# Dummy products ahead of the first transposes, 256-column key-value products and weight splitting on GpSimd in a hybrid decoder layer

## The chip, the cores and the metric

The kernel runs on one core of one Trainium2 chip. The metric is device time in microseconds, from the start to the end of one execution. A core has five engines with queues of their own: TensorE (PE, with its weight loads as PEld), VectorE (DVE), ScalarE (ACT), GpSimd (POOL) and SyncE (SP), which here only issues DMAs. PE multiplies from the on-chip memory SBUF into the eight banks of PSUM.

## The reference

One decoder layer on x of 1024 rows and 1024 columns, all in float32:

```
h  = rms_norm(x, pre_g);  z = h @ w_in            # 1024 x 7184
qa, ka, va, ga, qb, kb, vb, gb, gk_low = split(z)
oa = (softmax(q1 k1^T) - lam * softmax(q2 k2^T)) @ va     # 8 heads, causal
oa = rms_norm(oa, subln_g) * 0.8 * silu(ga)
ob = gated linear attention(qb, kb, vb, gk_low)           # 4 groups, chunks
ob = rms_norm(ob, gla_g) * silu(gb)
out = x + rms_norm(concat(oa, ob) @ w_out, post_g)
```

## The kernel before, in words

**Split products.** A large product runs on float32r operands: each is split into a high part, rounded by an ACT copy into a float32r tile, and a low part, the rest, subtracted by DVE. Three matmuls (high x high, low x high, high x low) make up one product. The linear attention's products of keys, values and state use plain float32 tiles.

**Start.** SP loads x in tiles of 128 rows. For tiles 0 to 3, `norm_x` (L486) squares a tile on ACT, makes the reciprocal root with `rstd` (L1477) on ACT and DVE, and scales the first 512 columns on DVE (L482) and the others on GpSimd. `first(0)` (L529) transposes the first halves on PE (L120) and `put` (L519) splits the result into high parts `h_hi` (ACT, L521) and low parts `h_lo` (DVE, L522); GpSimd adds them back as `f1` (L542). `first(1)` does the same for the second halves. `blocks` (L550) transposes rows 512 to 1023 (tiles 4 to 7, normalised in two groups of two) and forms the sums and differences s1 to s4 of the blocks of h.

**Input projection.** The product with `w_in` goes by one level of Strassen-Winograd: for each pair of 128 columns (`pairs`), seven products n = 1 to 7. `order` is the list of (pair, n); `go` (L595) walks it, `step` (L420) multiplies and evacuates one, and `prepare` (L238) makes the split weights three products ahead: a subtraction of raw weight blocks where n needs one (DVE, L296), the high part (ACT, L315), the low part (DVE, L316). Pairs of values are "wide": two pairs share one set of weights.

**The out-projection's weights.** During pairs 6 and up, `wo_step` (L580) splits `w_out`, one piece of 128 x 512 at a time. At n = 2 and 4 it loads a piece into the one raw tile (L592, SP), at n = 1 and 6 it makes the high part on ACT (L584) in a buffer of the four-buffer ring `c`, the low part on DVE in place (L586), and stores both to DRAM through SP (L588). The same ring serves the outputs of products 2, 7 (two) and 3.

**Linear attention.** `gla` (L758) is interleaved with the later products, one part per product: masked scores (mask on GpSimd, L775), transposed keys, keys times values (`kv`, L794), outputs (`gpo`), norm and gate.

**Afterwards** come the attention with the rest of the out-projection, ordered by the planner `merge` (L950), and the final rows (`finish`, L1436).

**Order.** PE's matmuls and transposes keep the program's order (L117, L120). Other engines' instructions are placed by a scheduler that simulates the timeline; `tc.keep_in_program_order` fixes an instruction's place among those fixed so on its engine, and `tc.issue_after` puts instructions behind a given one. Each engine works through its queue in order.

Of the kernel before, what the change touches and what calls it, by code (L numbers as in the profile page):

```python
# [8 lines left out]
F32 = mybir.dt.float32  # L9
F32R = mybir.dt.float32r  # L10
# [21 lines left out]
def hymba_kernel(  # L32
# [18 lines left out]


    nc = tc.nc
    act, dve, pool, pe, sp = nc.scalar, nc.vector, nc.gpsimd, nc.tensor, nc.sync

    def fp(t):
        return t.bitcast(F32)
# [2 lines left out]
        return slice(half * 512, half * 512 + 512)  # L60


    const = ctx.enter_context(tc.tile_pool(name="const", bufs=1))
    pre_g = const.tile([P, KT], F32, name="pre_g")
# [4 lines left out]
    ones = const.tile([P, P], F32R, name="ones")  # L69
    pool.memset(fp(ones), 1.0)  # L70

    NZ = 512
    maskt = const.tile([P, NZ + P], F32, name="maskt")
    pool.memset(maskt, 0.0)
# [46 lines left out]

    edge = ctx.enter_context(tc.tile_pool(name="edge", bufs=1, side="right"))
    pool.memset(edge.tile([P, 120], F32, name="edge"), 0.0)
    hw = ctx.enter_context(tc.tile_pool(name="hw", bufs=1, side="right", reuse_waits="tile"))
    hpool_cm = tc.tile_pool(name="hpool", bufs=1, side="right")
    hpool = hpool_cm.__enter__()

# [108 lines left out]
    def prepare(i):  # L238

        if i >= len(order) or i in ws:  # L240
            return
        if i < 4:

            act_ins, dve_ins = normed[0][:2]
            with tc.issue_after(act_ins.ins), tc.issue_after(dve_ins.ins):
                make_weights(i)
        else:
            make_weights(i)
# [69 lines left out]

    LEFT = {1: "h11", 2: "h12", 3: "s4", 4: "h22", 5: "s1", 6: "s2", 7: "s3"}
    NRING = 5  # L320

    def multiply(i, ps, start):
        p, n = order[i]
# [157 lines left out]
        x_cs = xs[st][:, cs]  # L481
        return engine.tensor_scalar(x_cs, x_cs, norms[st], 1.0, ALU.mult, ALU.mult)  # L482

    norms, normed = {}, []

    def norm_x(*sts):  # L486
        n = len(sts)
        ssq = const.tile([P, 4, n], F32, tag=f"ssq{sts[0]}", name="ssq", bufs=1)
        for i, st in enumerate(sts):
            junk = hw.tile([P, D], F32, tag=("s2_hi0", "s2_lo0")[st % 2], name="junk")  # L490
            ins = act.activation(
                junk, xs[st], AF.Square, scale=D**-0.5, accum_out=ssq[:, 0, i : i + 1]
            )
            if n == 1:
                tc.keep_in_program_order(ins)
        pin = tc.keep_in_program_order if n == 1 else None
        normed[:] = [rstd(nc, ssq[:, :, :n], ssq[:, 0, :n], eps_t, pin)]
        for i, st in enumerate(sts):
            norms[st] = ssq[:, 1, i : i + 1]
            if n == 1:  # L500
                pin(scale_x(st, cols(0), dve))
            else:
                scale_x(st, slice(0, D))

# [6 lines left out]
    load_raw(1)  # L511
    load_early(2)
    load_early(4)
    for st in range(4):
        norm_x(st)
    for st in range(4):
# [12 lines left out]
    def first(h):  # L529

        ps = [take_bank([P, 512], "xT") for _ in range(HB)]
        for i in range(4):
            for j in range(HB):
                k = h * HB + j
                tr(ps[j][0][:, i * P : (i + 1) * P], xs[i][:, k * P : (k + 1) * P])
        hi, lo = H[("h11", "h12")[h]]
        for j in range(HB):
            put(ps[j][0], h * HB + j, (hi, lo), j)
            if h:
                act.activation(f1[h][:, j], ps[j][0], AF.Copy, scale=pre_g[:, h * HB + j : h * HB + j + 1])  # L540
            else:
                pool.tensor_tensor(f1[h][:, j], fp(at(hi, j)), fp(at(lo, j)), ALU.add)  # L542
            free.append(ps[j][1])
# [36 lines left out]
    def wo_step(n):  # L580
        if n in (1, 6) and wo_open:
            e, dh, raw = wo_open.pop()
            hi = t_c("wo_hi", F32R)
            act.copy(hi, raw)  # L584
            lo = raw.bitcast(F32R)
            dve.tensor_tensor(lo, raw, fp(hi), ALU.subtract)  # L586
            for t, src in enumerate((hi, lo)):
                sp.dma_start(wod[e][t][:, cols(dh)], fp(src))  # L588
        if n in (2, 4) and wo_todo:
            e, dh = wo_todo.pop(0)  # L590
            raw = ap.tile([P, 512], F32, tag="t4", name="wo_raw", bufs=1)
            sp.dma_start(raw, w_out[0, e * P : (e + 1) * P, cols(dh)])  # L592
            wo_open.append((e, dh, raw))

    def go(n):  # L595
# [10 lines left out]
            if fill and next(fill[0], 0) == 0:  # L606
                fill.pop(0)

    prepare(0)
    first(0)  # L610
    for i in range(1, 4):
        prepare(i)
    go(1)
    first(1)
    go(2)
    norm_x(4, 5)
    norm_x(6, 7)
    go(1)
    for j in range(HB):
        blocks(j)  # L620
        go(1)
# [96 lines left out]


    sp.dma_start(sub_g, attn_subln_g[0].rearrange("(p o) -> p o", o=1))  # L720
    dve.tensor_scalar(sub_g, sub_g, 1.0 - LAM_INIT, None, ALU.mult)
# [36 lines left out]
    def gla(g):  # L758

        u = None  # L760
        for half in range(2):
# [215 lines left out]
    def pin(first, ins):  # L977

        if first:
            tc.keep_in_program_order(ins)  # L980
# [545 lines left out]
```

## Time and profile before

| | |
|---|---|
| median of 3 runs | 980.15 us (979.73 to 980.77) |
| the profiled execution | 979.08 us |
| its span, first to last instruction | 977.4 us |
| mean granted TensorE clock | 0.999 |
| HBM traffic over the span | 228 GB/s |

A row of the timeline begins with the start and the duration in us, then engine, line, operation, what is written from what, and a count where like instructions are merged; brackets tell how long the engine was idle before it, and what released it. A row of the chain is start, duration, engine and tile. A row of the waits is engine, tile and line, what it waited for, then total us, number and longest. A row of the windows has the stretch, its length, then busy us (with count) of PE, PEld, DVE, ACT and POOL or of PE alone, granted clock, busy share of the DMA engines and GB/s. A row of one tile's instructions gives minimum, median and maximum duration in ns, and the first and last start. A row of DMA issues ends with the size and the median us from issue to landing.

### The profile page before, as it was taken

Reading aid. Unit: us, or ns where it says so; the run is one execution under the profiler, and the core shown is the slowest. Engines: PE = TensorE matmul, PEld = TensorE weight load, DVE = VectorE, ACT = ScalarE, POOL = GpSimd, SP = SyncE. Lnnn points to the kernel's source line nnn. Section 1 sums busy time; section 2 is a strip of 40 time slices with the busy share of each in tenths; the row PEclk is TensorE's granted clock in tenths of the full one; section 3 lists DMA queues with packets and bytes.
Section 4 is the critical chain, followed back from the end, with each engine's and each line's share of the span. In section 5 each row is a group of like instructions: output and inputs, shape, how many; then the busy total and the mean of one; then the engine's idle time right before and its main releaser. Section 6 shows DMA issues by size and latency. Waiting matters only on the chain.

```text
span 977.4 us, 15766 instructions
## 1 busy us (share of the span) xinstructions
PE 956.7 (98%) x5338; PEld 830.4 (85%) x5338; DVE 735.4 (75%) x1452; ACT 600.5 (61%) x1164; POOL 142.9 (15%) x158
## 2 busy tenths in 40 slices
PE   5999999999999999999999999999999999999997
PEld 5998988888889998999888888878888888888785
DVE  6887597789866667686786876487888888898554
ACT  8742455487357455454665775366776687887773
POOL 4300000000000010000200002121322222443321
PEclk9999999999999999999999999999999999999999
DMA  9432446656774868897987866987656669994677
GB/s 345 151 110 91 139 135 205 231 179 225 238 247 162 264 187 286 254 294 229 293 259 243 273 202 191 407 269 272 197 186 228 240 199 344 340 294 105 151 208 147
DMA packets 152593, 220.45 MB, mean 226 GB/s; under 512 B 17104, under 2 KB 83664, under 8 KB 152416
## 3 DMA queue, kind: packets, MB, share of 16 engines
q1 hardware_dynamic: 146176, 203.71, 64.1%
q0 software_dynamic: 6336, 15.73, 7.0%
q8 instruction: 42, 0.69, 0.3%
q14 instruction: 39, 0.32, 0.1%
HBM read 133.93 MB, written 88.60 MB: 228 GB/s over the span
## 4 chain that ended last, share of the span: by engine, by line
PE 95%; DVE 2%; ACT 1%; DMA 1%; issue 1%; POOL 0%; SPq 0%; DVEq 0%; ACTq 0%; POOLq 0%
PE x L117 24%; PE y L117 15%; PE z L117 15%; PE ypart L117 13%; PE sc L117 7%; PE po L117 5%; PE yps L117 4%; PE wtr L120 3%; PE gpo L117 3%; PE kv L117 1%; PE gkl_ps L117 1%; PE pa L117 1%; DMA x<-in_x_dram 1%; PE xT L120 1%; DVE s_lo L548 0%
## 5 line engine op out<-in xcount | busy, mean ns | idle before, releaser
L315 ACT CAST w<-w_raw 128x512 fp32r<-128x512 f32 (+1 forms) x164 | 112.4, 688 | 94.7 <-PE y L117 44.1
L316 DVE TENSOR_TENSOR w<-w_raw,w 128x512 fp32r<-128x512 f32 (+1 forms) x164 | 126.7, 774 | 50.1 <-ACT w L315 43.3
L1049 ACT ACTIVATE p<-p,stt 128x896 f32<-128x896 f32 (+7 forms) x128 | 99.3, 777 | 36.7 <-DVE stt L1039 33.9
L427 ACT COPY s<-x 128x512 f32<-128x512 f32 x84 | 49.1, 585 | 84.4 <-PE x L117 84.3
L775 POOL TENSOR_SCALAR_AFFINE_SELECT gan<-gan 128x512 f32<-128x512 f32 x8 | 16.5, 2060 | 485.4 <-ACT gan L774 449.8
L296 DVE TENSOR_TENSOR w_raw<-w_raw 128x512 f32<-128x512 f32 (+1 forms) x96 | 75.9, 791 | 13.9 <-DMA w_raw<-in_w_in_dram 12.6
L1039 DVE CUSTOM_DVE_ANT_0 p<-sc,maskt 128x512 f32<-128x512 f32 (+3 forms) x128 | 74.3, 585 | 14.5 <-PE sc L117 13.3
L117 PE MATMUL ypart<-wo_hi,m_hi 128*128 128x512 f32 x192 | 79.5, 414 | 0.1
L117 PE MATMUL y<-h_hi,w 128*128 128x512 f32 x320 | 79.6, 391 | 0.0
L117 PE MATMUL z<-s_hi,w 128*128 128x512 f32 x320 | 79.6, 391 | 0.0
L117 PE MATMUL x<-s_hi,w 128*128 128x512 f32 x320 | 79.6, 391 | 0.0
L1055 POOL TENSOR_SCALAR p<-p,stt,lam 128x1024 f32<-128x1024 f32 (+3 forms) x64 | 56.2, 879 | 146.9 <-DVE stt L1054 141.9
L117 PE MATMUL ypart<-wo_hi,m_lo 128*128 128x512 f32 x192 | 75.5, 393 | 0.0
L117 PE MATMUL ypart<-wo_lo,m_hi 128*128 128x512 f32 x192 | 75.4, 393 | 0.0
L117 PE MATMUL sc<-k,q 128*128 128x512 f32 (+1 forms) x192 | 69.0, 363 | 1.3 <-DVE stt L1039 1.2
L117 PEld LDWEIGHTS x<-s_hi,w 128*128 128x128 f32 x320 | 59.7, 188 | 12.2
L117 PEld LDWEIGHTS y<-h_hi,w 128*128 128x128 f32 x320 | 59.6, 188 | 12.2
L117 PEld LDWEIGHTS z<-s_hi,w 128*128 128x128 f32 x320 | 59.5, 188 | 12.0
L117 PE MATMUL sc<-ks,q 128*128 128x512 f32 (+1 forms) x192 | 66.1, 347 | 0.0
L1097 ACT CAST wt_hi<-wtr 128x512 fp32r<-128x512 f32 (+1 forms) x80 | 42.7, 534 | 24.6 <-PE wtr L120 23.8
L1098 DVE TENSOR_TENSOR wt_lo<-wtr,wt_hi 128x512 fp32r<-128x512 f32 (+1 forms) x80 | 50.7, 633 | 8.6 <-ACT wt_hi L1097 8.0
L1058 DVE SCALAR_TENSOR_TENSOR p<-p,stt,p 128x1024 f32<-128x1024 f32 (+3 forms) x64 | 52.1, 814 | 4.1 <-POOL p L1055 3.9
(226 smaller groups left out, 2247.7 us busy)
## 6 DMA issues: line engine op xcount, KB each, us to landing
w_raw<-in_w_in_dram SPq DMA_DIRECT2D x56, 512.0 KB, 4.7
wo_raw<-in_w_out_dram SPq DMA_DIRECT2D x32, 256.0 KB, 3.0
wo_d<-wo_hi SPq DMA_DIRECT2D x32, 256.0 KB, 2.8
wo_d<-wo_raw SPq DMA_DIRECT2D x32, 256.0 KB, 3.8
q<-q_d SPq DMA_DIRECT2D x32, 256.0 KB, 4.7
k<-k_d SPq DMA_DIRECT2D x32, 256.0 KB, 5.7
ks<-k_d SPq DMA_DIRECT2D x64, 128.0 KB, 6.2
v<-v_d SPq DMA_DIRECT2D x16, 512.0 KB, 7.0
```

The costliest lines, as they stand in the source:

```text
L117: tc.keep_in_program_order(pe.matmul(*a, **k))
L120: tc.keep_in_program_order(pe.transpose(dst, src, ident))
L296: dve.tensor_tensor(dst, a, b, ALU.subtract)
L315: act.copy(w[0], src)
L316: dve.tensor_tensor(w[1], src, fp(w[0]), ALU.subtract)
L427: act.copy(b[k], ps)
L1039: ins = dve.tensor_tensor_reduce(p[:, a:e], sc[:, : e - a], maskt[:, NZ + P - (e - a) :] if last else maskt[:, : e - a], 1.0, 3e38 if i == ...
L1049: act.activation(p[:, :n], p[:, :n], AF.Exp, bias=st[:, m : m + 1], scale=-1.0, accum_out=st[:, 2 + m : 3 + m],)
L1055: pool.tensor_scalar(p1[:, :n], p1[:, :n], st[:, 5:6], lam, ALU.mult, ALU.mult)
L1058: dve.scalar_tensor_tensor(p0[:, :n], p0[:, :n], st[:, 4:5], p1[:, :n], ALU.mult, ALU.subtract)
L1097: act.copy(hi[:, :n], pt[:, :n])
L1098: dve.tensor_tensor(lo[:, :n], pt[:, :n], fp(hi[:, :n]), ALU.subtract)
```

## The change

1. Two tiles, ones (128 x 128) and zeros (128 x 512, in the buffer that s1's first high part takes later), are set first on GpSimd. `spin(n)` accumulates n products of them into a PSUM bank that is taken last. In `first(0)`, 14 stand ahead of the first transposes and 3, 7, 3 and 4 behind the four groups of transposes.
2. ACT, DVE and GpSimd instructions keep the program's order from the first `norm_x` to the last `put` of `first(1)`. In this stretch the order of the program is now: prepare four products, `first(0)`, norms of tiles 4 to 7, product 1, `first(1)`, products 2 to 4. Weights 4 to 10 of `order` are issued behind the last instruction kept so on ACT and on DVE.
3. `kv` is one product of 256 columns in place of two of 128.
4. `wo_step` runs on GpSimd: copy, subtraction, and all three DMA issues.

```diff
+    class Queue:
+        def __init__(self, engine):
+            self.engine = engine
+        def __getattr__(self, name):
+            op = getattr(self.engine, name)
+            def run(*a, **k):
+                ins = op(*a, **k)
+                if pinned[0]:
+                    tc.keep_in_program_order(ins)
+                    self.last = ins.ins
+                return ins
+            return run
+    act, dve, pool = Queue(nc.scalar), Queue(nc.vector), Queue(nc.gpsimd)
...
+    ones = const.tile([P, P], F32R, name="ones")
+    pool.memset(fp(ones), 1.0)
+    idle = hw.tile([P, 512], F32R, tag="s1_hi0", name="idle")
+    pool.memset(fp(idle), 0.0)
...
-        if i < 4:
-            act_ins, dve_ins = normed[0][:2]
-            with tc.issue_after(act_ins.ins), tc.issue_after(dve_ins.ins):
+        if 4 <= i <= n_early:
+            with tc.issue_after(act.last), tc.issue_after(dve.last):
                 make_weights(i)
...
+    spins = []
+    def spin(n):
+        if not spins:
+            spins.append(bank(free[-1], [P, 512], "spin"))
+        for i in range(n):
+            mm(spins[0], ones, idle, start=(i == 0), stop=(i == n - 1))
...
+    pinned[0] = True
     for st in range(4):
         norm_x(st)
...
     def first(h):
         ps = [take_bank([P, 512], "xT") for _ in range(HB)]
+        if not h:
+            spin(14)
         for i in range(4):
             for j in range(HB):
                 k = h * HB + j
                 tr(ps[j][0][:, i * P : (i + 1) * P], xs[i][:, k * P : (k + 1) * P])
+            if not h:
+                spin((3, 7, 3, 4)[i])
         hi, lo = H[("h11", "h12")[h]]
         for j in range(HB):
             put(ps[j][0], h * HB + j, (hi, lo), j)
+        pinned[0] = not h
...
-            act.copy(hi, raw)
+            pool.tensor_copy(hi, raw)
             lo = raw.bitcast(F32R)
-            dve.tensor_tensor(lo, raw, fp(hi), ALU.subtract)
+            pool.tensor_tensor(lo, raw, fp(hi), ALU.subtract)
             for t, src in enumerate((hi, lo)):
-                sp.dma_start(wod[e][t][:, cols(dh)], fp(src))
+                pool.dma_start(wod[e][t][:, cols(dh)], fp(src))
...
-            sp.dma_start(raw, w_out[0, e * P : (e + 1) * P, cols(dh)])
+            pool.dma_start(raw, w_out[0, e * P : (e + 1) * P, cols(dh)])
...
-    prepare(0)
+    for i in range(4):
+        prepare(i)
     first(0)
-    for i in range(1, 4):
-        prepare(i)
-    go(1)
-    first(1)
-    go(2)
     norm_x(4, 5)
     norm_x(6, 7)
     go(1)
+    first(1)
+    go(3)
...
-                    for t in range(2):
-                        mm(
-                            kv[:, i, t * P : (t + 1) * P], kn[:, 2 * m + i, :],
-                            v[:, t, 2 * m + i, :], start=True, stop=True,
-                        )
+                    mm(
+                        kv[:, i].rearrange("p (t c) -> p t c", c=P), kn[:, 2 * m + i, :],
+                        v[:, :, 2 * m + i, :], start=True, stop=True,
+                    )
```

More of the change, by code (lines that the diff above doesn't have):

```diff
@@ L53, in hymba_kernel @@
     nc = tc.nc
-    act, dve, pool, pe, sp = nc.scalar, nc.vector, nc.gpsimd, nc.tensor, nc.sync
+    pe, sp = nc.tensor, nc.sync
+    pinned = [False]
+    class Queue:
[11 more added lines that the diff above has]
+    act, dve, pool = Queue(nc.scalar), Queue(nc.vector), Queue(nc.gpsimd)
     def fp(t):
@@ L60, in cols @@
         return slice(half * 512, half * 512 + 512)
+    edge = ctx.enter_context(tc.tile_pool(name="edge", bufs=1, side="right"))
+    hw = ctx.enter_context(tc.tile_pool(name="hw", bufs=1, side="right", reuse_waits="tile"))
     const = ctx.enter_context(tc.tile_pool(name="const", bufs=1))
+    ones = const.tile([P, P], F32R, name="ones")
+    pool.memset(fp(ones), 1.0)
+    idle = hw.tile([P, 512], F32R, tag="s1_hi0", name="idle")
+    pool.memset(fp(idle), 0.0)
+    pool.memset(edge.tile([P, 120], F32, name="edge"), 0.0)
     pre_g = const.tile([P, KT], F32, name="pre_g")
@@ L68, in hymba_kernel @@
     pool.memset(eps_t, EPS)
-    ones = const.tile([P, P], F32R, name="ones")
-    pool.memset(fp(ones), 1.0)
     NZ = 512
@@ L120, in tr @@
         tc.keep_in_program_order(pe.transpose(dst, src, ident))
-    edge = ctx.enter_context(tc.tile_pool(name="edge", bufs=1, side="right"))
-    pool.memset(edge.tile([P, 120], F32, name="edge"), 0.0)
-    hw = ctx.enter_context(tc.tile_pool(name="hw", bufs=1, side="right", reuse_waits="tile"))
     hpool_cm = tc.tile_pool(name="hpool", bufs=1, side="right")
@@ L482, in scale_x @@
         return engine.tensor_scalar(x_cs, x_cs, norms[st], 1.0, ALU.mult, ALU.mult)
-    norms, normed = {}, []
+    norms = {}
     def norm_x(*sts):
@@ L490, in norm_x @@
             junk = hw.tile([P, D], F32, tag=("s2_hi0", "s2_lo0")[st % 2], name="junk")
-            ins = act.activation(
+            act.activation(
                 junk, xs[st], AF.Square, scale=D**-0.5, accum_out=ssq[:, 0, i : i + 1]
             )
[L494 to L497, printed above, removed]
+        rstd(nc, ssq[:, :, :n], ssq[:, 0, :n], eps_t, tc.keep_in_program_order)
         for i, st in enumerate(sts):
@@ L500, in norm_x @@
             if n == 1:
-                pin(scale_x(st, cols(0), dve))
+                scale_x(st, cols(0), dve)
             else:
@@ L538, in first @@
             put(ps[j][0], h * HB + j, (hi, lo), j)
+        pinned[0] = not h
+        for j in range(HB):
             if h:
@@ L720, in hymba_kernel @@
     sp.dma_start(sub_g, attn_subln_g[0].rearrange("(p o) -> p o", o=1))
-    dve.tensor_scalar(sub_g, sub_g, 1.0 - LAM_INIT, None, ALU.mult)
+    tc.keep_in_program_order(dve.tensor_scalar(sub_g, sub_g, 1.0 - LAM_INIT, None, ALU.mult))
     sp.dma_start(gla_g, gla_norm_g[0].rearrange("(t p) -> p t", p=P))
```

## The prediction

> **What bounds the kernel now.** I read the page's busy shares first, then what TensorE (PE) waited for, the chain that ended last, and busy time by stage.
>
> ```profile
> span 977.4 us, 15766 instructions
> ...
> PE 956.7 (98%) x5338; PEld 830.4 (85%) x5338; DVE 735.4 (75%) x1452; ACT 600.5 (61%) x1164; POOL 142.9 (15%) x158
> ```
>
> ```profile
> PE xT L120 <- DVE x L482: 9.4, 4, 7.2
> PE y L117 <- DVE s L565: 1.3, 1, 1.3
> ```
>
> ```profile
> 14.41 5.76 PE x L117 x24
> 20.17 1.75 PE xT L120 x16
> 21.91 2.88 PE x L117 x24
> 24.79 5.76 PE y L117 x48
> ...
> 41.83 0.69 DVE gv_st L403
> ...
> 58.09 1.23 DVE w L316
> ...
> 59.37 5.06 PE x L117 x40
> ```
>
> ```profile
> 150.00:275.00 125.00, 125.00 (x553) 103.52 (x552) 102.46 (x165) 70.73 (x123) 0.00 (x0) 1.00 0.66 219
> 275.00:560.00 285.00, 285.00 (x1801) 257.95 (x1800) 203.41 (x311) 163.10 (x285) 16.48 (x8) 1.00 0.78 248
> ```
>
> PE is the bound: 956.7 of 977.4 us. Its longest wait is 9.4 us ahead of the first transposes, which follow each other at the pace of normalised rows. The chain shows two other things. The first product (24 matmuls) takes 5.76 us and the next, of the same shape, 2.88: 240 against 120 ns each. And from 41.83 to 59.37 the chain runs over DVE: there a microsecond saved on PE survives only if DVE is early too. From 150 to 560, where the out-projection's weights are split, PE (second number of each row) is busy all the time: nothing taken off ACT or DVE there can shorten the run, and something added can lengthen it.
>
> **Part 1: dummy products, and the pinned order.**
>
> ```profile
> 18.45 1.72 PE L117 MATMUL x<-w,h_lo 128*128 128x256 f32 x8
> 20.01 1.91 PE L120 MATMUL xT<-ident,x 128*128 128x128 f32 x16
> ...
> 23.67 1.12 PE L117 MATMUL x<-w,h_lo 128*128 128x256 f32 x8
> ```
>
> ```profile
> 15.00:20.00 5.00, 5.00 (x23) 1.00 1.06 392
> ```
>
> ```profile
> 2.19 0.28 POOL L75 TENSOR_SCALAR_AFFINE_SELECT maskt<-maskt 128x128 f32<-128x128 f32 x1
> ...
> 16.17 5.99 POOL L542 TENSOR_TENSOR f1hi<-h_hi,h_lo 128x512 f32<-128x512 f32 x4 [2.95 <-DVE h_lo L522]
> ```
>
> ```profile
> 11.60 2.17 ACT L315 CAST w<-w_raw 128x1024 fp32r<-128x1024 f32 x2
> 13.68 2.42 ACT L521 ACTIVATE h_hi<-xT,pre_g 128x512 fp32r<-128x512 f32 x4
> 15.97 1.07 ACT L491 ACTIVATE junk<-xt 128x1024 f32<-128x1024 f32 x1
> ...
> 21.62 2.42 ACT L521 ACTIVATE h_hi<-xT,pre_g 128x512 fp32r<-128x512 f32 x4 [0.21 <-PE xT L120]
> ```
>
> ```profile
> 12.66 2.77 DVE L316 TENSOR_TENSOR w<-w_raw,w 128x1024 fp32r<-128x1024 f32 x2
> 15.35 2.71 DVE L522 SCALAR_TENSOR_TENSOR h_lo<-xT,pre_g,h_hi 128x512 fp32r<-128x512 f32 x4
> ...
> 19.14 1.88 DVE L296 TENSOR_TENSOR w_raw<-w_raw 128x1024 f32<-128x1024 f32 x1 [0.42 <-DMA w_raw<-in_w_in_dram]
> ...
> 22.17 1.21 DVE L296 TENSOR_TENSOR w_raw<-w_raw 128x1024 f32<-128x1024 f32 x1
> ...
> 29.68 1.23 DVE L316 TENSOR_TENSOR w<-w_early,w 128x1024 fp32r<-128x1024 f32 x1 [1.28 <-DMA out_dram<-in_x_dram]
> ...
> 32.32 0.75 DVE L522 SCALAR_TENSOR_TENSOR h_lo<-xT,pre_g,h_hi 128x512 fp32r<-128x512 f32 x1 [0.81 <-ACT h_hi L521]
> ```
>
> The same eight low-part matmuls take 1.72 us at 18.45 and 1.12 at 23.67, with all inputs there: the array is slow for about 5.5 us after its steady work begins at 14.41, then twice as fast. The granted clock (third number of the window's row) is 1.00 all along and doesn't show it. Fourteen dummies of 512 columns at the slow rate (240/256 x 512, at most 480 ns) fill some 6 us from about 2 us on (GpSimd's small setup operations end at 2.5 now, and the zeros move to their front), and 3, 7, 3 and 4 more fill the gaps between transposes. So the array should be fast before 14.41. The four last ones end before it: fast transposes end near 13.2 and four times 0.24 us reaches 14.2.
>
> The first product then isn't 2.88 us shorter. Its start stays: the first high part waits for ACT's two casts, which end at 13.68 in the pinned order too. Its last third needs DVE's low parts, whose last ends at 15.35 + 2.71 = 18.06. It ends at 18.06 + 2 x 0.12 = 18.3 instead of 20.0: 1.7 us earlier. Next comes ACT. Between 15.97 and 21.62 it has only 0.21 us idle; four squares, two Ln and Exp pairs and one copy out of PSUM stand in this stretch, and the pinned order leaves all of them ahead of the second half's high parts. These end near 21.62 + 2.42 = 24.04 as before. The third product now arrives at 22.9, needs the last of them for its seventh matmul, and ends no earlier than 24.04 + 18 x 0.12 = 26.2; its predecessor ended at 24.79 + 2.88 = 27.67 on the chain, 27.5 by start of the next. That leaves 1.3 us, less some 0.2 because Ln and Exp now stand in line: **-1.1 us**.
>
> Does DVE keep it? Two subtractions (L296 at 19.14 and 22.17) must now wait until the last pinned low part, about 25, and cost 2 x 1.21 = 2.4 us. DVE idles 1.28 + 0.81 = 2.1 us before 32.32, which holds nearly all of it, so it enters its full stretch about a microsecond early and the chain's later pieces move along. Bounds: -2.9 (5.76 - 2.88, nothing downstream interferes) and +1.3 (the 2.4 us fall into the full stretch, less 1.1). I take -1.1, the nearest to the rows. Moving memsets forward costs nothing: PE's first real work is at 7.2.
>
> **Part 2: keys times values.**
>
> ```profile
> 282.54 5.44 PE x L117 x24
> 287.98 1.78 PE kv L117 x16
> ```
>
> ```profile
> L117 PE MATMUL kv<-gv,gan x112: 270/275/275, 287.8 to 550.3; 128*128 128x128 f32 x112
> ```
>
> ```profile
> L117 PE MATMUL sc<-k,q x192: 218/389/502, 632.4 to 902.6; 128*128 128x512 f32 x99, 128*128 128x384 f32 x32, 128*128 128x256 f32 x31, 128*128 128x128 f32 x30
> ```
>
> The code makes 56 calls (4 groups, 7 tiles, 2 halves of the values) and the trace has 112 rows: a call on plain float32 runs as two matmuls, 1.78/16 = 111 ns each, 12.5 us in all. With 28 calls of 256 columns there are 56. At the rate of the products (120 ns for 256 columns) they would cost 6.7 us, saving 5.8. But those run on fp32r. The score products have 128-column forms on fp32r too, and their shortest row is 218 ns against 270 for the shortest here: 52 ns more, what 128 columns cost at 120/256 each. So a float32 row costs two passes, and 256 columns 2 x 107 = 213 ns plus 4 to 13 of overhead: 56 x 0.217 to 0.226 = 12.2 to 12.7 us. I take **-0.1**, bounds -5.8 and +0.2. The Trainium skill speaks against this edit too: FP8 and Floating Point Precision, TensorE Precision Notes, has true FP32 as four passes through the array. By that, too, cost follows columns and the saving is nil; the two rows of two passes agree.
>
> **Part 3: weight splitting on GpSimd.**
>
> ```profile
> 652.86 0.77 POOL L1055 TENSOR_SCALAR p<-p,stt,lam 128x512 f32<-128x512 f32 x1 [1.58 <-DVE stt L1054]
> ```
>
> ```profile
> 693.34 1.30 POOL L1147 TENSOR_TENSOR gate<-r,gate 128x512 f32<-128x512 f32 x1 [2.15 <-DVE stt L1054]
> ```
>
> ```profile
> wo_raw<-in_w_out_dram SPq DMA_DIRECT2D x32, 256.0 KB, 3.0
> wo_d<-wo_hi SPq DMA_DIRECT2D x32, 256.0 KB, 2.8
> wo_d<-wo_raw SPq DMA_DIRECT2D x32, 256.0 KB, 3.8
> ...
> y_d<-yst SPq DMA_DIRECT2D x16, 256.0 KB, 4.4
> ...
> y_d<-yst POOLq DMA_DIRECT2D x16, 256.0 KB, 5.1
> ```
>
> 32 casts leave ACT, 32 subtractions leave DVE, 96 DMA issues leave SP; worth nothing, since PE never waits there. The question is whether GpSimd keeps up. One raw tile serves all, so a cycle is load, cast, subtract, issue, store. GpSimd's DMAs land 5.1 - 4.4 = 0.7 us later at this size: 3.7 + 0.77 + 1.4 + 0.5 + 4.5 = 10.9 us (bounds 8.2, everything at SP's times, and 13.3, both DMAs at 5.1, subtraction 1.5, issue 0.8). PE uses two per pair of seven products of 5.44/2 = 2.72 us: one per 9.5 us, until 275, when linear attention thins them out. The backlog is 1.4 us a cycle over ten cycles, 13.8 us. The slack: a high part sits in a ring of four buffers, whose turn comes round nine products (24.5 us) after the last holder's product; that holder leaves at 4.2, the high part stays 6.2: 14.1 us. It just fits. Beyond it DVE would stand at the tile that reuses the buffer, with the next weights' low parts queued behind; these are made three products ahead, of which I count two, 5.4 us, as cover. So **0 us**. Behind a waiting GpSimd stands only the causal mask, needed five products (13.6 us) after it is issued. GpSimd also slows DVE: beside its four additions from 16.17 to 22.16 a subtraction took 1.88 us against 1.21 alone. At 2.2 us of arithmetic in 10.9 that hits a fifth of DVE's work, up to 11%, where DVE is 102.46 of 125 us busy and gives a subtraction away per cycle: no bound yet. By the Trainium skill (DMA: Bandwidth & Descriptors, Anatomy of one DMA, SWDGE path) 256 KB take 2.0 + 0.6 = 2.6 us; this is shorter than the 5.1 of the row here, and with it the cycle would be about 7.9 and the doubt gone. I stay with the row.
>
> **Sum.** -1.1 - 0.1 + 0 = -1.2 us on an execution of 979.08 (span 977.4). The median of the runs is 980.15, 1.1 above it; I put the change on the median: **979.0**, own range 976.9 to 981.5.
>
> **Rivals.**
> - *GpSimd falls behind* (0.15). From a cycle of about 11.5 us the backlog passes slack and cover; at 12.0 it is 24.8 us over ten cycles, less 14.1 and 5.4: +5.3, so 984.3; at 13.3 it would be +18. For: in the present order the loop runs at nearly PE's pace. Against: a GpSimd that does nothing else never waits for ACT or DVE.
> - *DVE's stall goes too* (0.10): PE keeps the whole 1.7 us and the 1.3 us wait for L565 vanishes as well: 977.1. For: DVE has two subtractions fewer behind it if they fit its idle time. Against: ACT's queue.
> - *256 float32 columns at the fp32r rate* (0.08): -5.8 more, 973.2. Against: the 270 ns.
> - *Dummies don't wake the array* (0.07): zeros count as idle, or a gap lets it fall back: 980.0.
>
> **How the numbers follow.** The forecast has 0.60. A measurement of this kernel tells about 0.2%, 2 us, from no change. Of the forecast's own range I give 0.18 to faster, 0.40 to same, 0.02 to slower; DVE's stall and float32 add 0.18 to faster; GpSimd adds 0.13 to slower, 0.02 to same; idle zeros 0.05 and 0.02. Faster 0.36, same 0.47, slower 0.17. The range runs from 973.0 (takes in the float32 rival) to 984.0 (the nearer half of GpSimd's).
>
> **What would show it.** Right: the first 24 matmuls still start near 14.4 and the transposes behind them at 18.3; the third product waits on h_hi; kv has 56 rows of about 220 ns; PE stays at 125.00 of 125.00 from 150 to 275. Wrong: matmuls still 213 ns apart at 15; kv rows at 120 ns; PE idle behind DVE or the c tiles between 200 and 300; L296 inside 32 to 59.

## The result, and the profile after

The changed kernel takes 985.20 us (median of 6 runs, 982.22 to 986.28), the kernel before 979.94 beside it on the same chip (6 runs, 979.08 to 980.77). The ratio is 1.0043, with a 95% interval of 1.0031 to 1.0055: slower, by 3.0 to 5.4 us. The profiled execution took 986.12 us, 7.04 more than that of before (979.08).

Nearly all ScalarE, VectorE and GpSimd rows of the changed kernel carry line L66, the wrapper that calls the engine; products are L141, transposes L144. The page's head:

```profile
span 984.2 us, 15717 instructions
...
PE 965.8 (98%) x5313; PEld 832.3 (85%) x5313; DVE 748.7 (76%) x1420; ACT 585.0 (59%) x1132; POOL 262.9 (27%) x319
```

VectorE gave 32 subtractions away and is busy 13.3 us longer than before (735.4). That is the first thing to explain. The two stretches in which the weights are split (second number: TensorE):

```profile
150.00:275.00 125.00, 121.72 (x534) 99.50 (x533) 102.59 (x147) 61.50 (x107) 43.02 (x55) 1.00 0.61 202
275.00:560.00 285.00, 283.90 (x1721) 254.03 (x1720) 207.96 (x288) 151.69 (x261) 90.36 (x108) 1.00 0.78 247
```

TensorE was full in both; now it idles 3.3 us in the first and 1.1 in the second. What it waits for:

```profile
PE x L141 <- ACT s L66: 3.1, 2, 2.1
...
PE y L141 <- DVE s L66: 1.4, 1, 1.4
PE gpo L141 <- DVE gu L66: 1.0, 1, 1.0
```

The 9.4 us ahead of the first transposes are filled with dummies. The wait for L565 (`DVE s`) is still there, and there are two new waits for ScalarE's copy out of PSUM, 0.98 us at 225.56 and 2.15 at 247.34. Setting matmul against matmul in the two traces by their starts gives where the time goes (at times of the trace of before): the changed kernel is 1.03 us ahead at 19.5, 0.13 ahead at 27.3, 0.10 behind at 44 and 0.4 at 212, then 1.7 behind at 224, 4.4 at 243, 6.1 at 520 and 6.8 at the end. The start of its chain:

```profile
1.52 6.15 PE L141 MATMUL spin<-idle,ones 128*128 128x512 f32 x14 [1.52 <-POOL idle L66]
...
14.85 3.20 PE L141 MATMUL x<-w,h_hi 128*128 128x256 f32 x16
17.89 1.17 PE L141 MATMUL x<-w,h_lo 128*128 128x256 f32 x8
...
27.13 0.50 PE L141 MATMUL y<-w,h_lo 128*128 128x256 f32 x2 [0.16 <-DVE h_lo L66]
...
44.09 2.15 PE L141 MATMUL y<-w,h_hi 128*128 128x256 f32 x16 [1.44 <-DVE s L66]
```

The low parts' eight matmuls take 1.17 us (1.72 before): the array is awake. The gain, 1.1 us at 20, goes at the third product, whose last matmuls wait for VectorE's `h_lo` (27.13): 0.04 us are left at 28. The wait in the last row takes another 0.13.

### The profile page after: what moved, and what is told of

It is laid out like the page before. It is cut to its first block, busy times and chain, and to the rows that moved or that the text cites. A ratio compares the mean times of both kernels' runs of the same rounds, so it can differ in the third digit from the quotient of the medians.

```text
span 984.2 us, 15717 instructions
## 1 busy us (share of the span) xinstructions
PE 965.8 (98%) x5313; PEld 832.3 (85%) x5313; DVE 748.7 (76%) x1420; ACT 585.0 (59%) x1132; POOL 262.9 (27%) x319
## 4 chain that ended last, share of the span: by engine, by line
PE 83%; DVE 8%; DMA 3%; ACT 3%; issue 2%; SPq 1%; POOL 0%; DVEq 0%; ACTq 0%; POOLq 0%
PE x L141 19%; PE ypart L141 13%; PE z L141 13%; PE y L141 12%; PE sc L141 7%; PE po L141 5%; PE yps L141 4%; PE wtr L144 3%; PE gpo L141 3%; DVE w L66 1%; PE kv L141 1%; DVE c L66 1%; DMA w_raw<-in_w_in_dram 1%; DVE b L66 1%; DMA gg_d<-c 1%
## 5 line engine op out<-in xcount | busy, mean ns | idle before, releaser
L66 DVE TENSOR_TENSOR w<-w_raw,w 128x512 fp32r<-128x512 f32 (+1 forms) x164 | 136.8, 837 | 56.3 <-ACT w L66 46.8
L66 ACT CAST w<-w_raw 128x512 fp32r<-128x512 f32 (+1 forms) x164 | 112.5, 688 | 97.7 <-PE y L141 40.8
L66 ACT ACTIVATE p<-p,stt 128x896 f32<-128x896 f32 (+7 forms) x128 | 99.3, 776 | 37.1 <-DVE stt L66 35.8
L66 ACT COPY s<-x 128x512 f32<-128x512 f32 x84 | 49.0, 585 | 90.3 <-PE x L141 90.1
L66 DVE TENSOR_TENSOR w_raw<-w_raw 128x512 f32<-128x512 f32 (+1 forms) x96 | 80.7, 841 | 24.0 <-DMA w_raw<-in_w_in_dram 22.5
L66 POOL CAST wo_hi<-wo_raw 128x512 fp32r<-128x512 f32 x32 | 29.4, 920 | 249.3 <-DMA q_d<-c 113.2
L66 POOL TENSOR_SCALAR p<-p,stt,lam 128x1024 f32<-128x1024 f32 (+3 forms) x64 | 56.1, 877 | 146.5 <-DVE stt L66 144.7
L66 DVE CUSTOM_DVE_ANT_0 p<-sc,maskt 128x512 f32<-128x512 f32 (+3 forms) x128 | 74.3, 584 | 15.2 <-PE sc L141 13.9
L141 PE MATMUL x<-s_hi,w 128*128 128x512 f32 x320 | 80.3, 393 | 3.1 <-ACT s L66 3.1
L141 PE MATMUL z<-s_hi,w 128*128 128x512 f32 x320 | 79.9, 392 | 0.1
L141 PE MATMUL y<-h_hi,w 128*128 128x512 f32 x320 | 79.9, 392 | 0.0
L141 PE MATMUL ypart<-wo_hi,m_hi 128*128 128x512 f32 x192 | 79.5, 414 | 0.1
L141 PE MATMUL ypart<-wo_hi,m_lo 128*128 128x512 f32 x192 | 75.5, 393 | 0.0
L141 PE MATMUL ypart<-wo_lo,m_hi 128*128 128x512 f32 x192 | 75.4, 393 | 0.0
L141 PEld LDWEIGHTS x<-s_hi,w 128*128 128x128 f32 x320 | 59.6, 188 | 16.6 <-ACT s L66 4.4
L141 PE MATMUL sc<-k,q 128*128 128x512 f32 (+1 forms) x192 | 69.0, 363 | 1.5 <-DVE stt L66 1.5
L141 PEld LDWEIGHTS y<-h_hi,w 128*128 128x128 f32 x320 | 59.8, 188 | 12.3
L141 PEld LDWEIGHTS z<-s_hi,w 128*128 128x128 f32 x320 | 59.3, 188 | 12.9 <-DVE c L66 0.9
L141 PE MATMUL sc<-ks,q 128*128 128x512 f32 (+1 forms) x192 | 66.1, 347 | 0.0
L66 DVE TENSOR_TENSOR c<-z,s 128x512 f32<-128x512 f32 x48 | 32.9, 685 | 34.2 <-ACT s L66 11.3
L66 ACT CAST wt_hi<-wtr 128x512 fp32r<-128x512 f32 (+1 forms) x80 | 42.8, 535 | 26.4 <-PE wtr L144 25.1
L66 DVE TENSOR_TENSOR wt_lo<-wtr,wt_hi 128x512 fp32r<-128x512 f32 (+1 forms) x80 | 50.6, 632 | 8.9 <-ACT wt_hi L66 8.4
```

What stands on the lines that cost most here:

```text
L66: ins = op(*a, **k)
L141: tc.keep_in_program_order(pe.matmul(*a, **k))
```

## The experiments

Times are medians, with the ratio to the kernel before on the same chip. "Ahead" and "behind" compare starts of matching matmuls with those of before, in the profiled executions.

### Which edit it is

**e1, the changed kernel without the split on GpSimd:**

```
-  pool.tensor_copy(hi, raw)
-  pool.tensor_tensor(lo, raw, fp(hi), ALU.subtract)
-  pool.dma_start(...)            # three transfers
+  act.copy / dve.tensor_tensor / sp.dma_start, as before
```

> The changed kernel with the out-projection's weights split as before (ACT, DVE, SP). Theory: the whole loss comes from the split on GpSimd, and its first load (GpSimd, at 2.30 us) also delays x at the start, so this runs at 978.5 to 979.9, products start at 14.4 again and PE has no stall between 200 and 250. Rival (the pinned order or the dummies cost it): stays near 984.

Measured: 980.44 us, ratio 1.0006 (0.9997 to 1.0014). That is above the 978.5 to 979.9 expected. It is 0.8 us ahead at 43 and 1.0 at 289, and loses 2.3 in one wait at 410 (below).

**e2, the split on GpSimd alone**, the kernel before with nothing but the edit just undone:

> The kernel before with only the weight split on GpSimd. Theory: 983 to 986, products start at 14.8, PE stalls of 3 us or more behind ACT between 150 and 560. Rival (pinned order or dummies): 980.

Measured: 984.54, ratio 1.0046 (1.0033 to 1.0059). The split alone costs what the whole change costs; the other edits come to nothing together.

### What in the split costs

**e3, arithmetic alone** (cast and subtraction on GpSimd, transfers on SyncE), and **e4, transfers alone** (the three transfers on GpSimd's queue, arithmetic as before):

```
+ pool.tensor_copy(hi, raw); pool.tensor_tensor(lo, raw, fp(hi), ALU.subtract)   # the one
+ pool.dma_start(...)  # the other, three times
```

> The kernel before with only the two arithmetic operations of the split on GpSimd, all DMAs on SP. If the subtraction beside DVE is what costs (DVE operations with two inputs are held up about 1 us by each GpSimd subtraction): 982 to 985, and DVE's busy time does not fall by the 22 us that left it. If the ring of four buffers is held too long by GpSimd's slower DMAs: 980.

> The kernel before with only the three DMAs of the split on GpSimd's queue, arithmetic on ACT and DVE. If the slower DMAs hold the ring: 982 to 985. If the arithmetic costs: 980 to 980.5, with the 0.4 us at the start from the first load.

Measured: 981.46, ratio 1.0017 (1.0009 to 1.0026); and 982.07, ratio 1.0019 (1.0007 to 1.0031). The first lies between its two forecasts (980, and 982 to 985). Each is a third to a half of the loss, and together they are most of it. The arithmetic falls 1.5 us behind by 233, in the stretch where the whole split falls behind; the transfers are 0.5 behind by 20 and lose 1.0 at 408 and 1.7 at 567, elsewhere. So the time of e4, though within the 982 to 985 that were expected if the transfers held the ring, doesn't show that: at 408 VectorE stands 4.85 us at a weight load, and at 567 ScalarE's queue is late because the split's own cast stood 5.54 us at its load. In the changed kernel that cast is GpSimd's, and nothing is lost at either place.

**e6, the cast alone on GpSimd**, `pool.tensor_copy(hi, raw)` for `act.copy`:

> The kernel before with the cast of the out-projection's weights alone on GpSimd; the subtraction stays on VectorE, the transfers on SyncE. The arithmetic together (cast and subtraction) gave 981.46 us against 979.83. Theory B (the subtraction with its two operands slows VectorE beside it, and that is the loss): no loss, 979.3 to 980.3; VectorE's excess beside GpSimd's instructions between 150 and 565 us stays under 5 us, where cast and subtraction had 25. Theory C (any arithmetic on GpSimd costs, since the high part comes later and is held longer): as with both, 981.0 or more.

Measured: 980.29, ratio 1.0006 (0.9995 to 1.0016); no loss that can be told, though at the upper edge of what was expected. (Its profiled execution, 981.35, loses nothing from 60 to 530 us and 1.7 at 534, where VectorE's subtraction of the split stands 5.45 us for GpSimd's cast.) For every VectorE instruction between 150 and 565 that overlaps a GpSimd instruction I took its duration less the median of the same form without such an overlap: 5.1 us in all here, 25.1 with cast and subtraction, 29.7 with the whole split, 32.0 in the changed kernel and 1.6 before. It is the subtraction, for the most part. The largest group of VectorE's rows shows it too (first before, then after; busy us, mean ns of one):

```profile
L316 DVE TENSOR_TENSOR w<-w_raw,w 128x512 fp32r<-128x512 f32 x138 | 94.6, 687 | 43.6 <-ACT w L315 43.1
```

```profile
L66 DVE TENSOR_TENSOR w<-w_raw,w 128x512 fp32r<-128x512 f32 x138 | 104.4, 760 | 46.9 <-ACT w L66 46.8
```

Means hide what happens, because most of the 138 meet no GpSimd instruction. Single rows of the split alone show it, on GpSimd, VectorE, ScalarE and TensorE:

```profile
238.50 0.78 POOL L584 CAST wo_hi<-wo_raw 128x512 fp32r<-128x512 f32 x1 [2.44 <-DMA wo_raw<-in_w_out_dram]
239.36 1.61 POOL L586 TENSOR_TENSOR wo_raw<-wo_raw,wo_hi 128x512 fp32r<-128x512 f32 x1
```

```profile
238.72 1.10 DVE L382 SCALAR_TENSOR_TENSOR c<-c,b 128x512 f32<-128x512 f32 x1
239.75 1.78 DVE L375 TENSOR_TENSOR c<-c,g 128x512 f32<-128x512 f32 x1
...
243.25 0.68 DVE L440 TENSOR_TENSOR c<-z,s 128x512 f32<-128x512 f32 x1
```

```profile
243.97 0.63 ACT L372 ACTIVATE g<-c 128x512 f32<-128x512 f32 x1 [4.47 <-DVE c L440]
...
245.16 0.57 ACT L427 COPY s<-x 128x512 f32<-128x512 f32 x1
```

```profile
245.78 2.12 PE L117 MATMUL x<-s_hi,w 128*128 128x512 f32 x8 [1.58 <-ACT s L427]
```

The cast ends at 239.28 and the VectorE instruction that started beside it at 239.82; the subtraction ends at 240.97 and VectorE's next at 241.53: each 0.55 us after GpSimd's end. VectorE doesn't run slower, it stands until GpSimd's instruction is through and does its own work then. The two took 1.5 us more than their 0.68 alone. VectorE's queue carries that to `c<-z,s`, ScalarE stands 4.47 us at the gate's activation that needs it, and the copy out of PSUM is queued behind: TensorE loses 1.58 us. The same part before:

```profile
234.65 0.69 DVE L382 SCALAR_TENSOR_TENSOR c<-c,b 128x512 f32<-128x512 f32 x1
...
235.86 0.69 DVE L375 TENSOR_TENSOR c<-c,g 128x512 f32<-128x512 f32 x1
236.46 0.69 DVE L440 TENSOR_TENSOR c<-z,s 128x512 f32<-128x512 f32 x1
237.06 0.68 DVE L383 TENSOR_TENSOR gqd<-c,dstep 128x512 f32<-128x512 f32 x1
```

There is a second reason for the late `c<-z,s`: its place. The scheduler orders VectorE and ScalarE anew when the split moves, and here `gqd<-c,dstep` and a subtraction of weights, 1.2 us, have come ahead of it. By these rows, either delay without the other would have left TensorE a wait of some 0.1 to 0.4 us (an estimate: 1.58 less 1.5, or less 1.2).

Is it the new order alone, then? e3 and e6 answer that. Of VectorE's 149 instructions in e3 from 150 to 275 us (the split's own left out), 142 follow each other as in e6 and only 133 as in the kernel before; in e6, 136 of 152 do as before. The two orders are nearly the same, and the difference is the engine of the subtraction. TensorE's stretch (e3, then e6):

```profile
150.00:275.00 125.00, 124.19 (x547) 102.17 (x546) 106.05 (x150) 64.29 (x111) 28.82 (x24) 1.00 0.64 213
```

```profile
150.00:275.00 125.00, 125.00 (x554) 103.52 (x553) 104.68 (x166) 63.82 (x109) 10.73 (x12) 1.00 0.67 218
```

With the cast alone TensorE never idles and loses nothing in this stretch; with the subtraction it falls 1.4 us back (one execution each; the two times differ by 1.1 us by their ratios, whose intervals overlap). The whole split changes the order more (122 of 146 as before in the changed kernel), and for it no run keeps the order. In the changed kernel 44 two-operand instructions of VectorE that began inside a GpSimd one took over 0.9 us between 150 and 565, and 41 of them ended 0.5 to 0.6 us after a GpSimd instruction did. Those with one operand in PSUM (`c<-y,s`, `h_lo<-xT`) keep their 0.68 to 0.74 us beside it. The Trainium skill has this rule (SBUF — State Buffer, SBUF: two separate sides): GpSimd and VectorE, when VectorE's instruction has two SBUF inputs, share a pair of ports, and whichever of them begins first holds it for its whole instruction while the other blocks. The rows agree.

**e5, the split alone with a buffer of its own for the high part:**

```
-  hi = t_c("wo_hi", F32R)
+  hi = ap.tile([P, 512], F32R, tag="woh", name="wo_hi", bufs=1)
-  ap.tile([P, 256], F32, tag="gu", name="gu", bufs=5)
+  ap.tile([P, 256], F32, tag="gu", name="gu", bufs=3)
```

> The kernel before with the whole split on GpSimd, as in the run of the split alone (984.54 us), but the high part of the out-projection's weights has a buffer of its own and no longer takes one of the ring of four that the products' tiles share; for the room, a ring of small state tiles that is used only from 287 us on has three buffers for five. Theory A (the ring is held too long by a slow GpSimd): TensorE's waits between 212 and 250 us go, its matmuls at 250 us stand under 1 us behind those of before instead of some 3, and the time falls to 981.5 or less. Theory B (a VectorE that is slowed down beside GpSimd's subtractions, with the copies out of PSUM queued behind what waits for it): the waits there stay, over 2 us at 250, and the time stays at 983.5 or more.

Measured: 986.25, ratio 1.0069 (1.0057 to 1.0081). Theory A's forecast fails: with the ring out of the way the time rises. But the theory isn't empty. Two of the changed kernel's waits have the ring in them:

```profile
244.79 0.69 DVE L66 TENSOR_TENSOR c<-z,s 128x512 f32<-128x512 f32 x1 [2.37 <-DMA gg_d<-c]
```

```profile
247.34 2.11 PE L141 MATMUL x<-s_hi,w 128*128 128x512 f32 x8 [2.15 <-ACT s L66]
```

```profile
521.67 0.69 DVE L66 TENSOR_TENSOR c<-z,s 128x512 f32<-128x512 f32 x1 [7.00 <-DMA wo_d<-wo_hi]
```

VectorE stands 2.37 us for a buffer of the ring that a store still reads, and no instruction of GpSimd's arithmetic lies in the 6 us before: this loss of TensorE's, the largest, goes over the ring. The store landed 5.3 us after its issue at 239.44; in e2 the same store took 3.1 us, and VectorE didn't wait for it. Why it was slow was not tried. At 521.67 VectorE stands 7.00 us for the store of the split's high part itself, and TensorE's wait of 0.98 us at 526.36 (`gpo`) follows. In all, from 150 to 565 us VectorE stands at a tile of the ring for a store eight times, 17.7 us, where it was three times and 3.4 us before; TensorE waits behind at least two of the eight.

In e5 TensorE's only wait from 150 to 275 is 1.0 us at 227, and its matmuls fall 1.6 us back from 77 to 250, for 2.7 in e2 (0.33 to 3.01). How much of the time the ring takes can't be read from e5, though, since three more things change in it. VectorE's order is another one again. The small state tiles lost two buffers, and behind 289 us, where these are used, e5 falls 2.6 us further back and e2 only 0.8; the two causes are not separated. And nothing paces the split any more: eleven of its 32 pieces come before 150 us, where e2 has none, and they reach into VectorE's first full stretch, 42 to 60 (GpSimd, VectorE):

```profile
51.37 6.55 POOL L586 TENSOR_TENSOR wo_raw<-wo_raw,wo_hi 128x512 fp32r<-128x512 f32 x1
```

```profile
57.28 1.19 DVE L548 TENSOR_TENSOR s_lo<-h,s_hi 128x512 fp32r<-128x512 f32 x1
```

Here GpSimd is the one that stands: six microseconds for a subtraction that needs 1.3, while VectorE's instructions follow each other without a gap. By 77 this run is 2.75 us behind, 1.8 of it since 44.

### The start

**e10, dummies and pinned order alone** (e1 with the old loop of 128 columns), and **e8, no dummies** (e1 with the calls of `spin` removed):

> The kernel before with the dummies and the pinned order, without the other two edits. If the start gains 1.0 us that lasts until 405 us and the wait at 410 us belongs to keys times values: ahead by 0.8 to 1.1 us to the end, 978.5 to 979.2. Rival (being early at 405 us is what meets the late weight load, whatever the columns): the gain goes at 410 us, 979.8 to 980.7, as with both edits (980.44).

> The changed kernel with the split of the weights undone (980.44 us) and without the dummy products; the pinned order and the 256 columns of keys times values stay. If the dummies wake the array: the first product takes 5.7 us again instead of 4.4, and the matmuls that follow it start 1.4 to 1.8 us later than with the dummies; by 45 us, where VectorE holds TensorE in both, 0.3 to 1.0 us are left of it, and the whole takes 980.5 to 981.5. If the dummies do nothing that lasts: 979.8 to 980.5.

Measured: 979.86, ratio 1.0003 (0.9993 to 1.0014); and 979.93, ratio 1.0001 (0.9993 to 1.0010). With dummies (e1) and without (e8) the same kernel is 1.0 us ahead and 0.1 us behind at 289: a difference of 1.1 us there, a little over the 0.3 to 1.0 expected at 45. It comes from one execution each, and the start varies by as much without dummies: in e6, whose start is that of before, the matmuls are 120 ns apart from 17.5 us on (before, from 19.9), and it is 1.3 us ahead at 30. The end doesn't keep the difference, which was not expected: at 410 us e1 loses 2.3 us and e8 only 1.1, so that e8 ends no later. In e10 nothing is lost at 410, against the rival; 0.6 us ahead at 44 melts in small steps, 0.2 at 817, and is 0.2 behind at the end. So its time is the rival's, its place neither's.

**Where the rest of the start's gain goes.** In the changed kernel VectorE's small operations of the norms of rows 4 to 7 stand ahead of the second half's low parts:

```profile
19.28 1.13 DVE L1517 TENSOR_TENSOR ssq<-ssq 128x2 f32<-128x2 f32 x1
20.45 1.22 DVE L1518 TENSOR_TENSOR ssq<-ssq 128x2 f32<-128x2 f32 x1
...
22.10 1.05 DVE L1517 TENSOR_TENSOR ssq<-ssq 128x2 f32<-128x2 f32 x1
23.18 1.06 DVE L1518 TENSOR_TENSOR ssq<-ssq 128x2 f32<-128x2 f32 x1
...
24.36 2.72 DVE L66 SCALAR_TENSOR_TENSOR h_lo<-xT,pre_g,h_hi 128x512 fp32r<-128x512 f32 x4
```

```profile
16.60 5.04 POOL L66 TENSOR_TENSOR f1hi<-h_hi,h_lo 128x512 f32<-128x512 f32 x4 [2.95 <-DVE h_lo L66]
22.02 2.22 POOL L66 TENSOR_SCALAR xt<-xt,ssq 128x1024 f32<-128x1024 f32 x2 [0.38 <-ACT ssq L1510]
```

256 elements in 1.1 us, four times: each begins inside a GpSimd instruction and ends with it (23.18 + 1.06 = 24.24, GpSimd's 22.02 + 2.22 = 24.24). Three kernels moved this order.

```
# e7: first(1) ahead of norm_x(4, 5) and norm_x(6, 7), on the kernel of e1
# e11, on e10: norms of two rows not pinned: rstd(..., pin if n == 1 else None),
#      and pinned[0] = False behind first(0): product 1 and first(1) are free as well
# e12, on e10: pool.tensor_tensor(f1[0][:, j], ...) x4 moved behind norm_x(6, 7)
```

> The changed kernel with the split of the weights undone (980.44 us), and the second half of the first block's conversion put ahead of the norms of rows 4 to 7, as in the kernel before. Theory B (the dummies' gain is lost because VectorE's small operations of these norms, 1.05 to 1.22 us each beside GpSimd's additions, stand ahead of the second half's low parts): the third product ends at least 1 us earlier than in that run, and TensorE's matmuls at 30 us stand 1.2 us or more ahead of before's; if nothing else waits for these norms, the whole takes 979.0 to 979.8. Rival (the low parts are late anyway, or the next transposes then wait for the norms): ahead by under 0.5 us at 45, 980.0 to 981.0.

> As the run of the start alone, but the norms of rows 4 to 7 are not pinned: the scheduler may put VectorE's small operations of these norms behind the second half's low parts. If these operations, 1.05 to 1.22 us each beside GpSimd's additions, are what delays the low parts: the third product ends 1 to 2 us earlier than in that run, and 0.5 to 1 us of it is left at 45 us. Rival (the conversion waits for ScalarE's high parts in any order, or the transposes of rows 4 to 7 then wait for the norms): no earlier at 45 us, or later.

Measured: 989.94, ratio 1.0103 (1.0088 to 1.0118); and 984.02, ratio 1.0042 (1.0028 to 1.0055). Both miss: the norms then come too late for the transposes of rows 4 to 7, and TensorE idles around 30 us (2.59 us for `POOL xt` in the first, and more behind it). The array then falls back to its slow rate (granted clock 0.50 from 34 to 40 us and from 32 to 35), so that the one is 8.1 us behind at 33 and the other 2.7.

> As the run of the start alone (979.86 us), but GpSimd's four additions for the first block stand behind its scaling of rows 4 to 7 instead of ahead of it. In the traces so far a VectorE instruction with two SBUF operands that starts while GpSimd is within one ends only after GpSimd's has: 0.02 us after it for 128x2, 0.55 us after it for 128x512, whatever it takes alone. By this theory the first two small operations of the norm of rows 4 and 5 (1.12 and 1.22 us, both ended with an addition) take 0.25 us or less; those of rows 6 and 7 stand beside the scaling and keep about 1.1 us, ending with it; the low parts of the second half start 1.5 us or more earlier (23.67 there), and VectorE's two-operand subtractions of weights between 26 and 32 us, beside the additions now, take up to 1.1 us more each and end 0.55 to 1.1 us after an addition. Rival (the small operations are slow for another reason, such as a busy SBUF in general): they keep 1 us without the additions. For the time: the low parts' gain of 1 us is given back at the weights' subtractions, 979.3 to 980.7; faster than 979.0 only if VectorE has room for both.

Measured: 983.46, ratio 1.0033 (1.0022 to 1.0044). The rows on VectorE, GpSimd and TensorE:

```profile
18.41 0.16 DVE L1519 TENSOR_TENSOR ssq<-ssq 128x2 f32<-128x2 f32 x1 [0.33 <-ACT ssq L1512]
...
22.13 2.73 DVE L66 SCALAR_TENSOR_TENSOR h_lo<-xT,pre_g,h_hi 128x512 fp32r<-128x512 f32 x4
24.77 1.99 DVE L66 TENSOR_TENSOR w_raw<-w_raw 128x1024 f32<-128x1024 f32 x1
26.68 2.32 DVE L66 TENSOR_TENSOR w<-w_early,w 128x1024 fp32r<-128x1024 f32 x1
```

```profile
24.38 7.99 POOL L66 TENSOR_TENSOR f1hi<-h_hi,h_lo 128x512 f32<-128x512 f32 x4
```

```profile
45.32 2.85 PE L141 MATMUL y<-w,h_hi 128*128 128x256 f32 x16 [2.85 <-DVE s L66]
```

```profile
46.00:48.00 2.00, 2.00 (x14) 2.00 (x13) 2.00 (x4) 0.00 (x0) 0.00 (x0) 0.61 0.00 0
48.00:50.00 2.00, 2.00 (x11) 1.96 (x10) 2.00 (x4) 1.08 (x2) 0.00 (x0) 0.53 0.00 0
```

Without additions beside them the two-operand small operations take 0.16 us, those of the second pair too, and the low parts start 1.5 us earlier (22.13 for 23.67 in the start alone). The additions now meet the weights' subtractions: 1.22 us becomes 1.7 to 2.3, four times, and an addition up to 2.28 instead of 1.28, the two taking turns. VectorE is late where it was late already, TensorE waits 2.85 us instead of 1.5, and pays again because its granted clock then falls to about half. The theory of the blocked instruction holds in both places; the expected time was 3 us too good.

### Keys times values

```
-  for t in range(2): mm(kv[:, i, t*P:(t+1)*P], ..., v[:, t, ...])
+  mm(kv[:, i].rearrange("p (t c) -> p t c", c=P), ..., v[:, :, ...])
```

> The kernel before with keys times values in 256 columns and nothing else. If the cost goes by columns (the rows of the changed kernel: 56 of about 220 ns): time as before, 979.2 to 980.2, and TensorE's matmuls at 405 us within 0.4 us of before's. Rival (this edit brings the wait at 410 us that the runs with the split undone show, where VectorE stands at a weight load that lands 1 us later and the linear attention's product behind it): 1.1 to 1.4 us behind from 412 us on, 980.5 to 981.3.

Measured: 980.52, ratio 1.0017 (1.0002 to 1.0031). The rival came true: 0.5 us ahead at 326 (its start happened to be early), 1.2 behind at 410. Of that, 0.7 goes at 365, in another wait for VectorE, and 0.9 at 410. There TensorE's product of the linear attention waits for `gu`, and VectorE, in order, stands ahead of it for a weight load (before, then this kernel):

```profile
407.62 1.23 DVE L296 TENSOR_TENSOR w_raw<-w_raw 128x1024 f32<-128x1024 f32 x1 [0.82 <-DMA w_raw<-in_w_in_dram]
```

```profile
409.48 1.23 DVE L296 TENSOR_TENSOR w_raw<-w_raw 128x1024 f32<-128x1024 f32 x1 [2.81 <-DMA w_raw<-in_w_in_dram]
```

The load is issued 0.9 us later (403.28 for 402.34) and lands 6.2 us after its issue instead of some 5. In e10, which loses nothing there, it takes 6.1 us as well, but is issued at 401.43. The wait is not this edit's alone: e4, e11 and e12, which don't have it, wait there too, and in the changed kernel, 4 us late by then, VectorE waits for the load but TensorE doesn't wait for VectorE. What delays the load is open; it wasn't tried.

## Why the prediction was wrong

It said 979.0, faster or the same with 0.83, and it was slower by 4.2 us by the ratio; the range ended at 984.0. The step that failed is in Part 3: that the split costs **0 us**. It costs 4.5 by the ratio of e2. Two readings carried the 0, and neither held: that GpSimd's slowing of VectorE "hits a fifth of DVE's work, up to 11%" and is "no bound yet", and that the ring's slack "just fits". The runs show both losses in rows; how the 4.5 us divide between them, the new order and the transfers stays open.

- **Part 3, the cycle: right.** Rows of the changed kernel: load, cast, subtraction, issue, store.

```profile
wo_raw<-in_w_out_dram POOLq DMA_DIRECT2D x32, 256.0 KB, 3.6
wo_d<-wo_hi POOLq DMA_DIRECT2D x32, 256.0 KB, 3.1
wo_d<-wo_raw POOLq DMA_DIRECT2D x32, 256.0 KB, 4.2
```

```profile
L66 POOL TENSOR_TENSOR wo_raw<-wo_raw,wo_hi 128x512 fp32r<-128x512 f32 x32 | 48.8, 1525 | 2.7
L66 POOL CAST wo_hi<-wo_raw 128x512 fp32r<-128x512 f32 x32 | 29.4, 920 | 249.3 <-DMA q_d<-c 113.2 <-DMA wo_raw<-in_w_out_dram 63.9 <-DVE c L66 21.2
```

  3.6 + 0.9 + 1.5 + 0.5 + 4.2 = 10.7 us, estimated at 10.9. The estimate of 2.6 us from the Trainium skill (DMA: Bandwidth & Descriptors, Anatomy of one DMA) is shorter than each of the three.
- **Part 3, the price beside VectorE: the first mistake.** The row that carried it (1.88 us beside four additions, 1.21 alone) was read as a rate, 1.55 times as long over a fifth of the work. It is one wait of up to a whole GpSimd instruction. Averaged over 125 us the rate isn't even bad: VectorE's busy time there is 102.59 us, as before (102.46), so what it gave away came back as waiting. But TensorE doesn't wait for an average. The waits fall on two or three instructions in a row, in a queue with a chain behind it: VectorE's sum, ScalarE's gate, ScalarE's copy out of PSUM, the next product. The prediction named VectorE's 102.46 of 125 us as room and did not follow who stands behind a late tile. That this alone costs time is shown by e3 against e6, 1.4 us up to 233; the rows of e2 at 238 to 246 show it together with the new order.
- **Part 3, the ring: the second mistake.** The rival "GpSimd falls behind" had the sign, the place and nearly the time (984.3). VectorE does stand at tiles of the ring (17.7 us in eight places), with its queue behind it, and two of TensorE's waits, 2.15 and 0.98 us, come of that. But the rival's condition, a cycle over 11.5 us and a growing backlog, is not what the medians show (10.7), and at 244.79 it was a store on SyncE's queue (`gg_d<-c`) that landed late; so its time is in part luck.
- **Part 3, transfers: sized in themselves, not in their order.** Alone on GpSimd's queue they cost 1.9 us by the ratio of e4, most of it at places where the changed kernel loses nothing. The first load is now issued ahead of the rows of x. The changed kernel's rows, then that of before:

```profile
2.30 0.74 POOL L66 DMA_DIRECT2D wo_raw<-in_w_out_dram  x1
```

```profile
8.81 1.06 ACT L66 ACTIVATE junk<-x 128x1024 f32<-128x1024 f32 x1 [1.01 <-DMA x<-in_x_dram]
```

```profile
8.38 1.06 ACT L491 ACTIVATE junk<-x 128x1024 f32<-128x1024 f32 x1 [0.63 <-DMA x<-in_x_dram]
```

  The third tile of x is squared at 8.39 to 8.81 in the four kernels that issue this load at about 2.2 us, at 7.61 to 8.38 in the ten others. So the rows of x seem to come later with it. That it moves the first product is not shown: this starts at 14.85 in the changed kernel, where the prediction said "its start stays" (14.41), but at 14.21, 14.21 and 13.98 in the other three with this load, and at 13.56 to 14.41 without it.
- **Part 1, -1.1: the size was met between e1 and e8 (1.1 us at 289 us), in part by luck,** since the start without dummies varies by as much (e6). The array was awake for the first product, as forecast. But the third product waits for VectorE's `h_lo`, not ScalarE's `h_hi`: the pinned order puts the small norm operations ahead of it, and the prediction, which counted ScalarE's part of these norms, left out VectorE's. In the changed kernel this took the whole gain. That the wait for VectorE at 44 us would keep nearly all of what reaches it was right: e1 is 0.95 us ahead in front of it and 0.81 behind it, e10 0.73 and 0.59.
- **Part 2, -0.1: right in itself.** 56 rows, 215 ns apart within a group (about 220 forecast):

```profile
L141 PE MATMUL kv<-gv,gan x56: 377/379/381, 292.4 to 556.4; 128*128 128x256 f32 x56
```

  The loss at 410 us, about 1 us when the edit is alone, was not foreseen; how the edit brings it is open.

No kernel here beats the one before.

## What to carry to other kernels

Before work goes to GpSimd, list the VectorE instructions that read two SBUF operands while it runs: each can stand for a whole GpSimd instruction, and what counts is who waits behind the one that stands, not the share of busy time. Do the same for every ring that a slower engine's tiles share with a faster one. A tight ring that holds an engine up may also be what keeps it away from a worse place. A gain at the head of a long in-order chain is kept only if every later meeting with a transfer or another queue has room for it; here 1.1 us came to nothing that could be measured.

## What the runs showed of the hardware

- A 128x2 operation on VectorE can take 1.2 us, 0.16 alone: it ended with the GpSimd instruction beside it. A VectorE instruction that begins first isn't stretched, and GpSimd stands instead (6.55 us for 1.3).
- TensorE's fast rate (dummies some 230 ns apart, not 427) came 2.7 us after the first dummy in e1 and over 5.7 us after it in the changed kernel. Idle times of that size lose it. After 2.85 us without work the granted clock fell to 0.53 to 0.61 for some 4 us (e12), which cost another 1.5 us. Two waits of 1.35 and 0.76 us with a matmul between them did it too (e11, clock 0.50). After the changed kernel's 2.15 us at 247 it did not fall. The Trainium skill (TensorE: Matmul & The Clock Gate, What's actually happening) gives a window of 3.4 us that runs on its own, and the slow state after at least one idle window. The scatter of the start fits that; the loss after 2.85 us, less than a window, does not, and here the measurement decides.
- At the start the granted clock reads 1.00 while matmuls are slow (213 ns for 256 columns at 15 us in the kernel before); later on it shows the slow rate (0.53 in e12).
